# Half of the taps of a depthwise convolution as column-tiled matmuls on shifted copies

## The chip, the cores and the metric

The kernel runs on one core of a Trainium2 chip. The core has a tensor engine (PE; its weight loads are listed apart as PEld), a vector engine (DVE), a scalar engine (ACT), GpSimd (POOL) and a sync engine (SP), which here issues the DMA transfers. The engines work side by side, each through its own list of instructions in order, and wait for one another by semaphores. Operands lie in SBUF, 128 partitions wide; matmul results go to PSUM.

The metric is the device time of one execution in microseconds, as the median of several runs. The profile is one further execution recorded by the hardware profiler.

## The reference

Four layers over a stream of 512 latent tokens and 256 context tokens with 1024 channels, in fp32. Layer i uses mixer i mod 3: layers 0 and 3 a Conformer convolution, layer 1 a two-way RWKV-7 scan, layer 2 attention. Each layer normalises and modulates its input and adds its gated result to the stream. The part that matters:

```python
def conv_branch(h, w_in, dw, db, ln_g, ln_b, w_out):
    a, b, gate = jnp.split(h @ w_in, 3, axis=-1)
    y = a * jax.nn.sigmoid(b)
    y = depthwise_conv(y, dw, db)          # 31 taps, each channel for itself
    y = jax.nn.silu(layernorm(y, ln_g, ln_b))
    return (y * jax.nn.silu(gate)) @ w_out
```

`h @ w_in` is 1024 x 3072 and `w_out` 1024 x 1024. Layer 0 does this for context and latent tokens; layer 3, whose context result nobody reads, for the 512 latent tokens alone.

## The kernel before, in words

Data stand channel-major: a tile is 128 channels by all tokens, and there are NT = 8 channel tiles. In layer 0 context and latent lie in one padded row, so that a convolution yields 783 positions a tile; in layer 3 it yields 512.

**Projections.** A projection of one column tile is a product of 8 chunks of 128 channels, each as three fp32r products (`whi·hhi`, `whi·hlo`, `wlo·hhi`, L175 to L182), for segments of 512 and, in layer 0, 256 tokens. Weights come by `wload` (L153): a DMA of 512 KB on SP's queue (L157) into one of two raw buffers, ACT rounds them to `whi` (L166), and another engine takes the rest to `wlo` (L168). In the convolution layers that is GpSimd. Results go to a ring of PSUM buffers, three in layer 0 and six in layer 3.

**The loop.** For each tile m the kernel projects b and a, takes tanh of b on ACT (L319), forms the gated product `yp` on DVE (L326), and convolves (L333 to L343). Of the 31 taps ACT does the first with the bias into `Y`, ACT makes the products of 4 to 8 further ones that GpSimd adds up in `a2` (L335 to L339), and DVE does the other 22 to 26, one multiply-add over the tile each (L341); at last `a2` is added (L343). After each projection two steps of a filler run: the modulation of layers 0 to 2, weight columns by DMA, groups of four 128x32 matmuls (L198) that stand side by side in the columns of the array, and small turning matmuls (L205).

**Behind the loop.** Gate projections and the layernorm's sums alternate in a fixed order (`GATE_ORDER`): silu on ACT (L353), the result to DRAM (L354), and matmuls with a matrix of 1/1024 for the channel mean of `Y` and of its square (L362, L364). Then come mean and deviation (L380 to L384) and for each tile subtraction on GpSimd (L392), three passes on DVE (L393, L396, L398) and two on ACT, and the output projection in eight columns, whose results DVE adds to the stream (L413).

**What sets the order.** The program is written tile by tile; a scheduler that simulates a timeline by its own costs fixes each engine's order beforehand. The scan of layer 1 has an order written out by hand, and is not touched.

Of the kernel before, what the change touches and what calls it, by code (L numbers as in the profile page):

```python
# [80 lines left out]
class Trunk:  # L81
# [14 lines left out]
    conv_names = ("dw_0", "conv_db", "conv_ln_g", "conv_ln_b")  # L96
# [75 lines left out]
    def mm3(self, segs, w, x, kt, m0=0, m=P, k0=0, first=True, last=True):  # L172
        """segs: [(psum ap, token slice)]; psum += w[:, k, m0:m0+m]^T x[k0 + k][:, tokens]"""
# [54 lines left out]
    def stat_add(self, m, s):  # L228
        """squares of channel tile m: the first tiles added up by GpSimd, the last two by the tensor engine"""
# [14 lines left out]
    def table(self, func, after):  # L244
        """the scalar engine's table for func, loaded as soon as the column `after` is there"""
# [22 lines left out]
    def normed(self, i, R, segs):  # L268
        """hi/lo of h = x*R*gs + shift"""
# [13 lines left out]
    # ---- Conformer convolution layer  # L283
    def conv_layer(self, i, j, lat_only, filler):
        nc, tc, I = self.nc, self.tc, self.I
        segs = self.segs_of(lat_only)
        lo_t = CTX if lat_only else 0
        ntok = TOK - lo_t
# [6 lines left out]
        # padded positions: ctx at PAD.., latent at PAD+CTX+PAD..; latent only: PAD..  # L295
# [1647 lines left out]
```

## Time and profile before

| | |
|---|---|
| median of 3 runs | 2635.33 us (2633.45 to 2638.43) |
| span of the profiled execution | 2633.3 us; its time outside the span is not recorded apart |
| PE, DVE, GpSimd, ACT busy | 2287.3, 1766.8, 1203.3, 1170.2 us |
| layer 0: first projection, end of the gates, end of the output | 42.9, 411.7, about 490 us |
| layer 3: first projection, last sum, end | 2304.9, 2556.4, 2633.3 us |
| DVE taps (L341), both layers | 364 of 1451 ns, 506.6 us |
| GpSimd adds of taps (L339), both layers | 100 of 2082 ns, 208.2 us |

The views used below: busy time of each engine in stretches of the span, with the clock that TensorE was granted; groups of instructions by line and shape, with count, busy time, mean duration and what ended the idle time before them; and the timeline of one engine, whose rows are start, duration, engine, line, operation, result and operands, and the number of instructions that the row holds. A matmul of fp32 over 512 positions shows as two records.

### The profile page before, as it was taken

What the parts mean: (1) busy time and instruction counts of PE and PEld (TensorE: products, weight loads), DVE (VectorE), ACT (ScalarE), POOL (GpSimd) and SP (SyncE); (2) the same over time, 40 slices, a digit from 0 to 9 for tenths busy, and PEclk for the clock granted to TensorE, in tenths of its full rate; (3) what the DMA queues carried; (4) which work ended last, traced back from release to release, by engine and by line L of the source; (5) the groups of instructions that cost most, each with busy time, mean ns of one, the idle gap of its engine ahead of it and who ended that gap; (6) DMA issues with size and microseconds to landing.
All of it is one profiled execution on the core that took longest, in us unless ns stands there. A gap on an engine that the chain in (4) does not pass through costs nothing. (4 is left out here: it accounts for less than half of the span.)

```text
span 2633.3 us, 42476 instructions
## 1 busy us (share of the span) xinstructions
PE 2287.3 (87%) x15987; PEld 1787.2 (68%) x15987; DVE 1766.8 (67%) x2839; ACT 1170.2 (44%) x2672; POOL 1203.3 (46%) x1116
## 2 busy tenths in 40 slices
PE   6976879699998798898988999989999999877637
PEld 4755558476667566566666677988899998765425
DVE  3899996778345777777776452546454555689993
ACT  4433335334344455565544543456455454433432
POOL 1565755534144445555531104445454444457652
PEclk9988889799999878898885799999999999998769
DMA  7543314245976544354431473111111112212212
GB/s 256 168 147 117 126 68 147 60 123 160 317 249 195 154 101 104 96 119 123 109 79 39 155 226 99 42 41 49 49 57 57 57 49 67 65 48 64 76 52 80
DMA packets 351421, 288.95 MB, mean 110 GB/s; under 512 B 106136, under 2 KB 301040, under 8 KB 351216
## 3 DMA queue, kind: packets, MB, share of 16 engines
q1 hardware_dynamic: 351216, 286.24, 36.6%
q8 instruction: 126, 2.06, 0.3%
q14 instruction: 79, 0.65, 0.1%
HBM read 222.11 MB, written 57.77 MB: 106 GB/s over the span
## 5 line engine op out<-in xcount | busy, mean ns | idle before, releaser
L168 POOL TENSOR_TENSOR wlo<-wraw,whi 128x1024 fp32r<-128x1024 f32 x136 | 362.6, 2670 | 331.3 <-ACT whi L166 285.5
L341 DVE SCALAR_TENSOR_TENSOR Y<-yp,VC,Y 128x783 f32<-128x783 f32 (+1 forms) x364 | 506.6, 1451 | 4.8 <-ACT Y L333 3.5
L166 ACT ACTIVATE whi<-wraw 128x1024 fp32r<-128x1024 f32 x168 | 176.3, 1052 | 211.9 <-DMA wraw<-in_attn_w_in_dram 42.6
L339 POOL TENSOR_TENSOR a<-a,a 128x783 f32<-128x783 f32 (+1 forms) x100 | 208.2, 2082 | 75.5 <-ACT a L335 64.6
L179 PE MATMUL cps<-hhi,whi 128*128 128x512 f32 x576 | 187.7, 383 | 33.3 <-ACT sg L353 15.1
L179 PE MATMUL cps<-hhi,wlo 128*128 128x512 f32 x576 | 185.1, 375 | 21.5 <-POOL wlo L168 21.5
L1696 PE MATMUL pj<-whi,hhi 128*128 128x256 f32 x640 | 182.6, 286 | 4.2 <-ACT junk L1705 2.6
L179 PE MATMUL cps<-hlo,whi 128*128 128x512 f32 (+1 forms) x576 | 185.0, 376 | 0.0
L1696 PE MATMUL pj<-wlo,hhi 128*128 128x256 f32 x640 | 182.0, 285 | 0.0
L1696 PE MATMUL pj<-whi,hlo 128*128 128x256 f32 x640 | 181.9, 285 | 0.0
L1207 POOL TENSOR_SCALAR SD<-VT,DC 64x64 f32<-64x64 f32 x160 | 66.2, 414 | 226.9 <-DVE VT L1230 183.2
L179 PEld LDWEIGHTS cps<-hhi,whi 128*128 128x128 f32 x576 | 102.5, 203 | 71.2 <-ACT sg L353 18.8
L1007 PE MATMUL pg<-ARP,BK 128*128 128x256 f32 x384 | 147.8, 480 | 3.0 <-DVE BK L991 2.6
L338 ACT ACTIVATE a<-yp,VC 128x783 f32<-128x783 f32 (+1 forms) x100 | 83.0, 834 | 120.5 <-POOL a L339 120.4
L179 PEld LDWEIGHTS cps<-hhi,wlo 128*128 128x128 f32 x576 | 102.1, 201 | 43.0 <-POOL wlo L168 23.6
L1696 PEld LDWEIGHTS pj<-whi,hhi 128*128 128x128 f32 x640 | 123.6, 193 | 5.4 <-ACT junk L1705 3.3
L1696 PEld LDWEIGHTS pj<-wlo,hhi 128*128 128x128 f32 x640 | 123.7, 193 | 0.7
L1696 PEld LDWEIGHTS pj<-whi,hlo 128*128 128x128 f32 x640 | 123.4, 193 | 0.1
L1230 DVE SCALAR_TENSOR_TENSOR VT<-c,DC,SD 64x64 f32<-64x64 f32 x320 | 90.2, 282 | 49.3 <-PE c L1218 25.8
L1112 DVE TENSOR_TENSOR tm<-inst,Ti 96x207 f32<-96x207 f32 (+10 forms) x240 | 105.1, 438 | 18.6 <-DMA inst<-gn 10.7
L179 PEld LDWEIGHTS cps<-hlo,whi 128*128 128x128 f32 x576 | 102.4, 202 | 21.8 <-issue 2.4
L921 ACT ACTIVATE VT<-c 64x64 f32<-64x64 f32 x384 | 83.3, 217 | 73.0 <-PE c L1211 65.3
(342 smaller groups left out, 6234.4 us busy)
## 6 DMA issues: line engine op xcount, KB each, us to landing
mraw<-in_mod_w_dram SPq DMA_DIRECT2D x36, 1024.0 KB
wraw<-in_conv_w_in_dram SPq DMA_DIRECT2D x48, 512.0 KB
wraw<-in_attn_w_in_dram SPq DMA_DIRECT2D x48, 512.0 KB
mraw<-in_mod_w_dram SPq DMA_DIRECT2D x24, 512.0 KB
F<-dF SPq DMA_DIRECT2D x24, 384.0 KB
KR<-dF SPq DMA_DIRECT2D x24, 384.0 KB
wraw<-in_conv_w_out_dram SPq DMA_DIRECT2D x16, 512.0 KB
wraw<-in_attn_w_out_dram SPq DMA_DIRECT2D x16, 512.0 KB
```

What stands on the lines that cost most here:

```text
L166: nc.scalar.activation(hi[:, :n], raw[:, :n], AF.Copy)
L168: lo_eng.tensor_tensor(out=lo[:, :n], in0=raw[:, :n], in1=hi.bitcast(F32)[:, :n], op=ALU.subtract)
L179: nc.tensor.matmul(ps, a[:, k, m0:m0 + m], b[k0 + k][:, ts], start=first and k == 0 and i == 0, stop=last and k == kt - 1 and i == 2)
L338: nc.scalar.activation(a3, yp[:, w_:w_ + nout], AF.Copy, scale=tap(w_))
L339: nc.gpsimd.tensor_tensor(out=a2, in0=a2, in1=a3, op=ALU.add)
L341: nc.vector.scalar_tensor_tensor(out=y, in0=yp[:, w_:w_ + nout], scalar=tap(w_), in1=y, op0=ALU.mult, op1=ALU.add)
L921: nc.scalar.activation(out, in_, AF.Copy)
L1007: nc.tensor.matmul(pg[u - u % 2][:, u % 2, :], BK[:, u].rearrange("p s t -> p (s t)"), ARP[:, :, u, :], start=True, stop=True)
L1112: eng("im", j).tensor_tensor(out=o, in0=inst[0:96, j, j + 1:32].unsqueeze(2).to_broadcast([96, n, c]), in1=Ti[0:96, j, 0:c].unsqueeze(1).t ...
L1207: eng("SD", 2 * d + k).tensor_scalar(out=SD[own], in0=src, scalar1=dc[own], scalar2=0.0, op0=ALU.mult, op1=ALU.add)
L1230: nc.vector.scalar_tensor_tensor(out=S, in0=pc[own, 2, :], scalar=dc[own], in1=SD[own], op0=ALU.mult, op1=ALU.add)
L1696: nc.tensor.matmul(o[:, n, :], a, b[:, k, :], start=kh == 0 and k == 0 and e == 0 and n == 0, stop=kh == 1 and k == 3 and e == 2 and n == 1)
```

## The change

Only the two convolution layers change, and the helpers that they call.

- `PE_TAPS = 16`: taps 0 to 15 are done on PE. `yp` of a tile is copied into `X` by 16 DMAs of 32 partitions on SP's queue, so that row 32g + r of chunk n holds channel 32n + r shifted by g. `W` holds the taps as diagonal weights; DVE makes it per tile as a product with four stacked unit matrices (`eye4`). `convolve` sums, for each chunk of 32 channels, four matmuls of K = 128 and M = 32 into that chunk's 32 PSUM partitions. `X` has one buffer.
- DVE keeps 14 taps a tile; tap 16 with the bias is ACT's. DVE adds the PSUM result to `Y` and keeps running sums of `Y` and its square, which two matmuls a segment average at the end.
- GpSimd adds nothing any more; all `wlo` splits of these layers are on DVE.
- Each gate projection stands inside the loop: b and a of tile m, the convolution of tile m - 1, the gate of tile m - 2.
- All normalising passes but ACT's are on DVE, and the first output columns are multiplied chunk by chunk while the tiles are normalised.

```diff
-GATE_ORDER = "g0 s0 s1 g1 s2 s3 g2 s4 g3 s5 g4 s6 g5 s7 g6 g7".split()
-POOL_TAPS = (8, 8, 8, 8, 8, 8, 6, 4)
+PE_TAPS = 16
+FIRST = 2
...
+        osegs = [(s, (olat if s == 0 else 0), t0, n) for s, t0, n in segs]
+        nq, nv = PE_TAPS // 4, CW - PE_TAPS
+        xw = nout + PE_TAPS - 4
...
+        for m in range(NT):
+            order += [("b", m), ("a", m)] + [("c", m - 1)] * (m > 0) + [("g", m - 2)] * (m > 1)
+        order += [("c", NT - 1), ("g", NT - 2), ("g", NT - 1)]
...
-                w = self.wload(w_in[:, part * D + m * P: part * D + (m + 1) * P], NT, P, nc.gpsimd)
...
+                w = ws.pop(0)
+                if cols[len(done) + 1:]:
+                    ws.append(self.wload(cols[len(done) + 1], NT, P, nc.vector))
...
-                yp = cv.tile([P, max(width, TOK)], F32, tag="yp", name="yp", bufs=3)
...
+                y = yp[m] = cv.tile([P, max(width, TOK)], F32, tag="yp", name="yp", bufs=2)
...
-                nc.scalar.activation(y, yp[:, 0:nout], AF.Identity, scale=tap(0), bias=bias)
-                a2 = cv.tile([P, nout], F32, tag="a2", name="a2")
-                nc.scalar.activation(a2, yp[:, 1:1 + nout], AF.Copy, scale=tap(1))
-                for w_ in range(2, 1 + npool):
-                    a3 = cv.tile([P, nout], F32, tag="a3", name="a3", bufs=2)
-                    nc.scalar.activation(a3, yp[:, w_:w_ + nout], AF.Copy, scale=tap(w_))
-                    nc.gpsimd.tensor_tensor(out=a2, in0=a2, in1=a3, op=ALU.add)
-                for w_ in range(1 + npool, CW):
-                    nc.vector.scalar_tensor_tensor(out=y, in0=yp[:, w_:w_ + nout], scalar=tap(w_), in1=y,
-                                                   op0=ALU.mult, op1=ALU.add)
-                nc.vector.tensor_tensor(out=y, in0=y, in1=a2, op=ALU.add)
+                X[m] = cv.tile([P, 4, xw], F32, tag="X", name="X")
+                for n in range(4):
+                    for g in range(4):
+                        nc.sync.dma_start(X[m][32 * g:32 * g + 32, n, :], y[32 * n:32 * n + 32, g:g + xw])
+                nc.scalar.activation(Y[m], y[:, PE_TAPS:PE_TAPS + nout], AF.Identity,
+                                     scale=self.vec("dw", nv)[:, m:m + 1], bias=self.vec("conv_db")[:, m:m + 1])
+                w = W[m] = cv.tile([P, nq, 4, 32], F32, tag="W", name="W", bufs=2)
+                nc.vector.tensor_tensor(out=w, in0=self.eye4.unsqueeze(1).unsqueeze(1).to_broadcast([P, nq, 4, 32]),
+                                        in1=self.WT.rearrange("p (q r) -> p q r", q=nq)[:, :, 4 * m:4 * m + 4].unsqueeze(3)
+                                        .to_broadcast([P, nq, 4, 32]), op=ALU.mult)
+                for v in range(1, nv):
+                    taps.append(lambda v=v: nc.vector.scalar_tensor_tensor(
+                        out=Y[m], in0=y[:, PE_TAPS + v:PE_TAPS + v + nout], scalar=self.vec("dw", nv)[:, v * NT + m:v * NT + m + 1],
+                        in1=Y[m], op0=ALU.mult, op1=ALU.add))
...
+            def convolve(m):
+                self.mark(f"L{i}conv")
+                p = self.big("yps")
+                for q in range(nq):
+                    for s, o, t0, n in osegs:
+                        for c in range(4):
+                            nc.tensor.matmul(p[32 * c:32 * c + 32, 512 * s:512 * s + n], W[m][:, q, c, :],
+                                             X[m][:, c, o + 4 * q:o + 4 * q + n], start=q == 0, stop=q == nq - 1)
+                def add():
+                    for s, o, t0, n in osegs:
+                        nc.vector.tensor_tensor(out=Y[m][:, o:o + n], in0=p[:, 512 * s:512 * s + n], in1=Y[m][:, o:o + n], op=ALU.add)
...
+                        nc.vector.tensor_tensor(out=sums[0], in0=sums[0], in1=Y[m], op=ALU.add)
+                        nc.vector.tensor_tensor(out=sums[1], in0=sums[1], in1=sq, op=ALU.add)
...
-                    nc.gpsimd.tensor_tensor(out=z[:, t0:t0 + n], in0=Y[m][:, o:o + n], in1=mean[:, c0:c0 + n], op=ALU.subtract)
...
+                    nc.vector.tensor_tensor(out=zz, in0=Y[m][:, o:o + n], in1=mean[:, c], op=ALU.subtract)
...
-            w = self.wload(w_out[:, m * P:(m + 1) * P], NT, P, nc.gpsimd)
...
+        load = lambda m: self.wload(w_out[:, m * P:(m + 1) * P], NT, P, nc.vector)
+        first = [(load(m), self.big("ops")) for m in range(FIRST)]
+        for k in range(NT):
+            make(k)
+            for w, ps in first:
+                self.mm3([(ps[:, 512 * s:512 * s + n], slice(t0, t0 + n)) for s, t0, n in segs], [a[:, k:k + 1] for a in w],
+                         ([y[0][k]], [y[1][k]]), 1, first=k == 0, last=k == NT - 1)
```

What stands where on the engines after the change, at three places. In a row the name ahead of the arrow is the result, those behind it the operands, numbered as the program makes them; line numbers are the changed kernel's (L188 is a projection matmul, L382 a convolution's, L207 and L214 the modulation's, L177 a split, L372 a tap, L166 a weight load, L364 a copy to X).

PE in layer 0, after the projection of a for tile 3 (`cps_1273`): the convolution of tile 2 (`X_1058`).

```order
L188 MATMUL cps_1273<-hhi_120,wlo_1195 128x512
L188 MATMUL cps_1273<-hhi_120,wlo_1195 128x256
L207 MATMUL mps_1254<-mraw_1322,sc_75 32x512 x4
L382 MATMUL yps_1371<-X_1058,W_1076 32x512 x4
L382 MATMUL yps_1371<-X_1058,W_1076 32x256 x4
L382 MATMUL yps_1371<-X_1058,W_1076 32x512 x4
L382 MATMUL yps_1371<-X_1058,W_1076 32x256 x4
L214 MATMUL mps_1330<-pick_77,mrow_1328 128x2 x4
```

Eight groups of four short matmuls a tile, four sets of taps by two segments, are new on PE there; they stand together, with steps of the modulation among them.

DVE in layer 0, first before, then after, from the gated product of a tile on (`Y1` to `Y3` are the tiles' sums, `VC` the taps).

```order
L326 SCALAR_TENSOR_TENSOR yp_1228<-th_1226,cps_1162 128x512
L326 SCALAR_TENSOR_TENSOR yp_1228<-th_1226,cps_1162 128x256
L341 SCALAR_TENSOR_TENSOR Y1_501<-yp_840,VC_409,Y1_501 128x783
L207 TENSOR_TENSOR modT1_68<-mps_1213,VT_78 128x8
L341 SCALAR_TENSOR_TENSOR Y2_502<-yp_1035,VC_409,Y2_502 128x783
L341 SCALAR_TENSOR_TENSOR Y1_501<-yp_840,VC_409,Y1_501 128x783
L341 SCALAR_TENSOR_TENSOR Y3_503<-yp_1228,VC_409,Y3_503 128x783
```
```order
L177 TENSOR_TENSOR wlo_1408<-wraw_1404,whi_1406 128x1024
L359 SCALAR_TENSOR_TENSOR yp_1345<-th_1343,cps_1273 128x512
L359 SCALAR_TENSOR_TENSOR yp_1345<-th_1343,cps_1273 128x256
L177 TENSOR_TENSOR wlo_1490<-wraw_1486,whi_1488 128x1024
L372 SCALAR_TENSOR_TENSOR Y3_509<-yp_1345,VC_411,Y3_509 128x783 x2
L216 TENSOR_TENSOR modT1_68<-mps_1330,VT_79 128x8
L372 SCALAR_TENSOR_TENSOR Y3_509<-yp_1345,VC_411,Y3_509 128x783
L220 SCALAR_TENSOR_TENSOR gs1_72<-modT1_68,VT_79 128x8
L372 SCALAR_TENSOR_TENSOR Y3_509<-yp_1345,VC_411,Y3_509 128x783 x2
L368 TENSOR_TENSOR W_1663<-eye4_78,WT_431 128x512
L386 TENSOR_TENSOR Y2_508<-yps_1371,Y2_508 128x512
```

Before, the taps of up to three tiles wait in DVE's list at once; after, those of one, with splits, a weight product and the add from PSUM between them.

SP in layer 3 (`X_23224` is tile 2's copy, `X_23382` tile 3's; the `wraw` rows are weight loads, SGD1 the store of a gate).

```order
L364 DMA X_23224<-yp_23220 32x524 x16
L166 DMA wraw_23499<-in_conv_w_in_dram 128x8x128
L166 DMA wraw_23579<-in_conv_w_in_dram 128x8x128
L404 DMA SGD1_22916<-sg_23459 128x512
L166 DMA wraw_23622<-in_conv_w_in_dram 128x8x128
L364 DMA X_23382<-yp_23378 32x524 x16
L166 DMA wraw_23659<-in_conv_w_in_dram 128x8x128
```

Sixteen copies a tile stand in SP's list between the weight loads, where before there were loads and stores of gates alone. On PE the convolution of a tile of layer 3 is split: three single matmuls of L382 between projection matmuls, then thirteen together.

More of the change, by code (lines that the diff above doesn't have):

```diff
@@ L303, in conv_layer @@
             Y = [cv.tile([P, nout], F32, name=f"Y{m}", tag=f"Y{m}") for m in range(NT)]
-            hx = self.hx
-            nn = 512 + (0 if lat_only else CTX)
-            def project(part, m):
-                w = self.wload(w_in[:, part * D + m * P: part * D + (m + 1) * P], NT, P, nc.gpsimd)
-                ps = self.big("cps")
-                self.mm3([(ps[:, 512 * s:512 * s + n], slice(t0, t0 + n)) for s, t0, n in segs], w, hx, NT)
+            sums = [cv.tile([P, nout], F32, name="sum0"), self.tp.tile([P, 783], F32, tag="acc", name="sum1", bufs=1)[:, :nout]]
@@ new lines, in glu, with total @@
+                for v in range(1, nv):
[5 more added lines that the diff above has]
+                p = self.big("yps")
+                for q in range(nq):
+                    for s, o, t0, n in osegs:
[5 more added lines that the diff above has]
+                        nc.vector.tensor_tensor(out=Y[m][:, o:o + n], in0=p[:, 512 * s:512 * s + n], in1=Y[m][:, o:o + n], op=ALU.add)
+                def total():
+                    sq = sums[1] if m == 0 else self.tp.tile([P, 783], F32, tag="sq", name="sqy")[:, :nout]
+                    nc.scalar.activation(sq, Y[m], AF.Square)
+                    if m == 0:
+                        nc.vector.tensor_copy(sums[0], Y[m])
+                    else:
+                        nc.vector.tensor_tensor(out=sums[0], in0=sums[0], in1=Y[m], op=ALU.add)
+                        nc.vector.tensor_tensor(out=sums[1], in0=sums[1], in1=sq, op=ALU.add)
+                taps.extend((add, total))
@@ L354, in gate @@
                 nc.sync.dma_start(SGD[m][:, lo_t:], sg[:, lo_t:])
                 return sg
-            def sums(m):
-                self.mark(f"L{i}ln")
-                sq = self.tp.tile([P, 783], F32, tag="sq", name="sqy")
-                nc.scalar.activation(sq[:, :nout], Y[m], AF.Square)
-                for s, o, t0, n in osegs:
-                    nc.tensor.matmul(pm[:, 512 * s:512 * s + n], self.mean_m, Y[m][:, o:o + n],
-                                     start=(m == 0), stop=(m == NT - 1))
-                    nc.tensor.matmul(pq[:, 512 * s:512 * s + n], self.mean_m, sq[:, o:o + n],
-                                     start=(m == 0), stop=(m == NT - 1))
@@ L367, in conv_layer @@
-            for x in GATE_ORDER:
-                if x[0] == "g":
-                    sg = gate(int(x[1:]))
-                else:
-                    sums(int(x[1:]))
+            for x, m in order:
+                if x == "c":
+                    convolve(m)
+                    if m == NT - 1:
+                        vector_work(len(taps))
+                    continue
+                project(x, m)
+                if x == "a":
+                    glu(m)
+                if x == "g":
+                    sg = gate(m)
@@ L403, in out_proj @@
+            self.out_proj(i, w_out, hx, segs, normalize)
+    def out_proj(self, i, w_out, y, segs, make):
         nc = self.nc
@@ L408, in out_proj, with finish @@
         late = []
-        def part(m, ps, w, segs):
-            self.mm3([(ps[:, 512 * s:512 * s + n], slice(t0, t0 + n)) for s, t0, n in segs], w, y, NT)
+        def finish(m, ps, segs):
             for s, t0, n in segs:
@@ L417, in part @@
                     self.stat_add(m, s)
-        for m in range(NT):
-            w = self.wload(w_out[:, m * P:(m + 1) * P], NT, P, nc.gpsimd)
+        def part(m, ps, w, segs):
+            self.mm3([(ps[:, 512 * s:512 * s + n], slice(t0, t0 + n)) for s, t0, n in segs], w, y, NT)
+            finish(m, ps, segs)
+        load = lambda m: self.wload(w_out[:, m * P:(m + 1) * P], NT, P, nc.vector)
[5 more added lines that the diff above has]
+                         ([y[0][k]], [y[1][k]]), 1, first=k == 0, last=k == NT - 1)
+        ahead = [load(m) for m in range(FIRST, FIRST + 1)]
+        for m, (w, ps) in enumerate(first):
+            finish(m, ps, segs)
+        for m in range(FIRST, NT):
+            w = ahead.pop(0)
+            if m + 1 < NT:
+                ahead.append(load(m + 1))
             ps = self.big("ops")
```

119 lines of the change are left out of this document (68 added, 51 removed).

## The prediction, as it was put on record

> **What bounds the kernel now.** I began with the page's busy times: no engine fills the span, and the chain of waits has only two trivial pieces, so it decides nothing. Next came busy time by stretch, laid over the two convolution layers (columns: length; PE, PEld, DVE, ACT, POOL busy; granted clock, DMA share, GB/s). The four rows of the second fence are layer 0, the one of the third is the middle of layer 3's loop.
>
> ```profile
> span 2633.3 us, 42476 instructions
> PE 2287.3 (87%) x15987; PEld 1787.2 (68%) x15987; DVE 1766.8 (67%) x2839; ACT 1170.2 (44%) x2672; POOL 1203.3 (46%) x1116
> ```
> ```profile
> 42.90:76.00 33.10, 31.53 (x195) 23.28 (x199) 16.89 (x38) 12.29 (x21) 1.99 (x10) 1.00 0.61 205
> ...
> 200.00:300.00 100.00, 70.11 (x370) 51.73 (x368) 100.00 (x75) 30.50 (x35) 58.77 (x31) 0.83 0.36 116
> ...
> 386.20:411.70 25.50, 25.50 (x146) 22.11 (x145) 20.30 (x17) 14.17 (x20) 14.93 (x12) 1.00 0.45 141
> ...
> 437.00:490.00 53.00, 50.75 (x278) 42.55 (x276) 14.67 (x28) 14.90 (x25) 25.08 (x33) 1.00 0.35 115
> ```
> ```profile
> 2400.00:2500.00 100.00, 66.89 (x213) 47.65 (x212) 100.00 (x88) 38.54 (x54) 67.38 (x42) 0.81 0.22 66
> ```
>
> In both loops DVE is busy for the whole stretch while PE is idle for a third of it at a granted clock near 0.8. Only at the end of layer 0's loop, where the last gate projections run, is PE the full one. So the taps on DVE set the loops. The groups of instructions say what a tap costs, and DVE's timeline says why:
>
> ```profile
> L341 DVE SCALAR_TENSOR_TENSOR Y<-yp,VC,Y 128x783 f32<-128x783 f32 x182 | 289.0, 1645 | 1.8 <-ACT Y L333 1.1
> L341 DVE SCALAR_TENSOR_TENSOR Y<-yp,VC,Y 128x512 f32<-128x512 f32 x182 | 217.6, 1258 | 3.0 <-ACT Y L333 2.4
> L343 DVE TENSOR_TENSOR Y<-Y,a 128x512 f32<-128x512 f32 x8 | 5.4, 680 | 0.1
> ```
> ```profile
> 119.70 8.58 DVE L341 SCALAR_TENSOR_TENSOR Y<-yp,VC,Y 128x783 f32<-128x783 f32 x9
> 128.20 0.97 DVE L343 TENSOR_TENSOR Y<-Y,a 128x783 f32<-128x783 f32 x1
> ...
> 130.01 9.92 DVE L341 SCALAR_TENSOR_TENSOR Y<-yp,VC,Y 128x783 f32<-128x783 f32 x4
> ...
> 2358.55 12.66 DVE L341 SCALAR_TENSOR_TENSOR Y<-yp,VC,Y 128x512 f32<-128x512 f32 x19
> ```
>
> The mean tap is 1.65 us in layer 0 and 1.26 in layer 3, but some runs of taps cost 0.95 (8.58/9) and 0.67 (12.66/19), others 2.5 (9.92/4). I read the difference as DVE sharing with GpSimd's adds and splits; the change takes both off GpSimd.
>
> **The change on DVE.** The price of a `wlo` split there stands in the rows of line 168, since some already run on DVE:
>
> ```profile
> L168 DVE TENSOR_TENSOR wlo<-wraw,whi x32: 1210/1225/2873, 544.3 to 1580.4; 128x1024 fp32r<-128x1024 f32 x32
> ```
>
> A tile of layer 0 is now 14 taps x 0.95 = 13.3 us, three splits 3.7, the gated product, the add from PSUM and two running sums about 1.0 each (0.97 in the row of 128.20), the weight product W 0.7 (680 ns, L343 at 512): 21.7 us. In layer 3 it is 14 x 0.67 + 3.7 + five operations of 0.68 = 16.5 us. If taps kept today's contended means, these would be 31.5 and 24.7 us.
>
> **The change on PE.** The convolution is new: groups of four 128x32 matmuls, each on its own 32 columns. Groups of that form exist today in the modulation (x8 is one group of four, two records each):
>
> ```profile
> 111.59 0.52 PE L179 MATMUL cps<-hhi,wlo 128*128 128x512 f32 x2
> 112.05 1.06 PE L198 MATMUL mps<-mraw,sc 128*32 128x512 f32 x8
> ...
> 113.49 0.51 PE L179 MATMUL cps<-hlo,whi 128*128 128x512 f32 x2
> 113.84 0.51 PE L179 MATMUL cps<-hhi,wlo 128*128 128x512 f32 x2
> ...
> 126.88 1.92 PE L198 MATMUL mps<-mraw,sc 128*32 128x512 f32 x16
> 128.73 0.62 PE L179 MATMUL cps<-hhi,whi 128*128 128x512 f32 x2
> ...
> 653.24 0.64 PE L198 MATMUL mps<-mraw,sc 128*32 128x256 f32 x8 [0.68 <-DMA mraw<-in_mod_w_dram]
> 653.81 1.12 PE L789 MATMUL pa<-AL,A 64*128 64x512 f32 x2
> ...
> 384.58 1.05 PE L364 MATMUL pq<-sqy,mean_m 128*128 128x512 f32 x2
> 385.46 0.59 PE L362 MATMUL pm<-Y,mean_m 128*128 128x256 f32 x2
> 385.89 0.59 PE L364 MATMUL pq<-sqy,mean_m 128*128 128x256 f32 x2
> ```
>
> From start to start: a projection pair (512 + 256 positions) is 0.35 us (113.49 to 113.84). A 512-wide group, back to back, is 0.93 ((128.73 - 126.88)/2), a 256-wide one 0.57. One group alone between projections is 1.2 (111.59 to 113.49 less two pairs), so a switch in and out costs 0.27. One full-array fp32 matmul of 512 is 0.88 (384.58 to 385.46), of 256 0.43. Four column tiles thus take about the time of one.
>
> By the Trainium skill, "TensorE: Matmul & The Clock Gate", section "Measured speedup vs the span model", three column tiles of 512 run 2.38 times as fast as in turn, 0.79 of the ideal; at that rate a group would be 1.11 us and the sum below 11 us longer. The row of 0.93 disagrees, so I keep the row.
>
> Layer 0, from 42.9: the rest of PE's work is modulation:
>
> ```profile
> L198 PE MATMUL mps<-mraw,sc 128*32 128x512 f32 x256 | 35.2, 644 | 0.4 <-DMA mraw<-in_mod_w_dram 0.4
> L205 PE MATMUL mps<-pick,mrow 128*128 128x2 f32 x136 | 21.9, 282 | 53.3 <-ACT mrow L202 43.7 <-DVE modT L207 9.2 <-DVE xl L1579 0.4
> ```
>
> 24 projections x 24 pairs x 0.35 = 201.6 us; 256/8 = 32 groups x 1.2 = 38.4; 136/8 = 17 turning groups at the 0.9 of other groups of eight fp32 records = 15 (their busy time today, much of it after a wait, is 21.9); convolutions 8 x (4 x (0.93 + 0.57) + 0.3) = 50. Sum 305 us, 38 per tile, against DVE's 21.7: PE becomes the bound, even if the contention stayed (31.5). For stalls I take 10 us (estimate): between none (386.20 row: 25.5 busy of 25.5) and 5% (42.90 row: 1.57 idle of 33.1). All gates then end at 42.9 + 315 = 358, today at 411.7.
>
> Behind it lies the layernorm, today partly beside the gates:
>
> ```profile
> 386.73 1.19 DVE L381 TENSOR_TENSOR rs<-pq,m 128x512 f32<-128x512 f32 x2 [3.09 <-ACT m L380]
> ...
> 389.80 4.96 DVE L384 RECIPROCAL rs<-rs 128x512 f32<-128x512 f32 x2 [1.89 <-ACT rs L382]
> ...
> 433.69 0.96 DVE L398 TENSOR_TENSOR hlo<-z,hhi 128x768 fp32r<-128x768 f32 x1 [0.91 <-ACT hhi L397]
> ...
> 2556.43 0.69 DVE L381 TENSOR_TENSOR rs<-pq,m 128x512 f32<-128x512 f32 x1 [3.94 <-PE pq L364]
> ...
> 2585.19 2.07 DVE L413 SCALAR_TENSOR_TENSOR xl<-ops,modT,xl 128x512 f32<-128x512 f32 x3 [2.16 <-PE ops L179]
> ```
>
> Mean matmuls, subtraction, root and reciprocal take 11 us (385.46 to 394.76 with 2 for matmuls), then 8 tiles x 4 passes of 0.95 to 1.1 = 33 us, all on DVE: the last `hlo` at 358 + 44 = 402, today 434.7. Three output columns run chunk by chunk under those 33 us (3 x 8.4 = 25); five remain, as in today's 437 to 490. Layer 0 gives 32 us. If nothing covered the first three columns, 25 of these go.
>
> Layer 3, whose projection pace is
>
> ```profile
> 2304.91 1.65 PE L179 MATMUL cps<-hhi,whi 128*128 128x512 f32 x3 [5.79 <-ACT hhi L278]
> ...
> 2313.19 0.39 PE L179 MATMUL cps<-hhi,wlo 128*128 128x512 f32 x1
> 2313.42 0.39 PE L179 MATMUL cps<-hlo,whi 128*128 128x512 f32 x1
> ```
>
> 0.2275 us (0.23 in these two rows): 24 x 24 x 0.2275 = 131 us. The order splits a convolution: three single column matmuls among the projections, then 13. I price a lone one at the full 0.88 + 0.2, between 0.23 (if it ran like one of a group) and 1.2; with 13/4 x 0.93 + 0.3 this is 6.5 us a tile, 52 in all. 183 us, plus 7 for the slow start and stalls, ends the loop at 2304.9 + 190 = 2495. The subtraction of L381 follows at about 2501 (last add, sums, mean matmuls), today 2556.4. Today 28.8 us lie between it and the first add to the stream (L413); after the change 4.9 us to the end of the reciprocal, 8 x 4 passes of 0.68 = 21.8 and 2.2 of PE make 28.9, so the part that GpSimd did costs DVE nothing on balance: without its contention the other passes shrink. The output columns stay. With 1.5 us of doubt, layer 3 gives 54 us.
>
> The new transfers fill X by 16 DMAs a tile on SP's queue, behind the weight loads, and X has one buffer: a refill starts when the previous convolution has ended. Nearest rows, two small DMAs on chip and the longest wait of such an issue:
>
> ```profile
> 826.81 0.42 SPq L1044 DMA_DIRECT2D gn<-GM  x1
> 827.28 0.43 SPq L1043 DMA_DIRECT2D gw<-GM  x1
> SPq L1045 <- DMA gn<-GM: 11.8, 26, 2.0
> ```
>
> 16 x 0.47 = 7.5 us of issue and 2.0 to land: 9.5 us. In layer 0 some 31 us of projections lie between two convolutions, in layer 3 45 matmuls (10.2 us) to the first chunk and 70 (16 us) to the last. I take it as hidden; the other bound is below. Behind a waiting refill SP holds the weight loads of the projections after the next, so a late refill would also delay PE's operands there. On DVE a `wlo` can stand behind six taps, 5.7 us in layer 0 and 4.0 in layer 3, while the projection that covers it lasts 8.4 and 5.5 us: it costs nothing, and up to 24 x 1.2 = 29 us in layer 3 if the cover were gone by one split.
>
> Together 32 + 54 = 86 us. The span, 2633.3, is 2.0 below the median of the runs; from the median 2635.3 - 86 = **2549 us**.
>
> **Rivals.**
>
> Transfers bound in layer 3. A tile moves 128 x 4 x 524 x 4 bytes = 1.07 MB besides 1.5 MB of weights. The page's mean is
>
> ```profile
> DMA packets 351421, 288.95 MB, mean 110 GB/s; under 512 B 106136, under 2 KB 301040, under 8 KB 351216
> ```
>
> and at 110 GB/s a refill takes 10 us alone and 20 with a weight load each side of it, 4 us past the last chunk's 16, seven times, so +28 us or less: 2575. For it: short packets of 2 KB. Against: 205 GB/s in the 42.90 row.
>
> Slower than before: the 16 transfers of a refill take turns instead of overlapping. At 2.0 us each that is 32 us, 16 more than layer 3 hides, x 7 = +112, and about 1 x 7 in layer 0: 2549 + 119 = 2668. It decides from a refill of 16 + 86/7 = 28 us. Against: the rows show issues 0.47 apart, and waits of 2.0 are the longest of 26.
>
> The column tiles don't run side by side, so the change doesn't do what it says. A group is then 4 x 0.88 = 3.5 and 4 x 0.43 = 1.7 us: +8 x 4 x (2.6 + 1.15) = 120 in layer 0 and 8 x 3.25 x 2.6 = 68 in layer 3: 2737. The rows of L198 speak against it; only that X and W are other operands is for it.
>
> A larger gain: lone matmuls at 0.3 instead of 1.08 (8 x 3 x 0.78 = 19), no stalls (17): 2513.
>
> **How the numbers follow.** Forecast 0.68, transfer-bound 0.13, larger gain 0.09, turns 0.05, column tiles in turn 0.02, a gain lost to several waits so that nothing is seen 0.03. Price errors of the forecast: -36 as in the larger gain, +17 if every group pays its switch (8 x 8 x 0.27), +15 for stalls at 5% of 488 us. The range goes from 2508 to 2594, the upper end holding the transfer case and both upper bounds in part. A difference of 0.2% (5 us) is what a measurement here can tell. Faster 0.90, same 0.03, slower 0.07.
>
> **What would show it.** Right: no GpSimd adds; taps near 0.95 and 0.67; PE nearly full in layer 0's loop at a clock near 1.0; the last gate near 358; the subtraction of L381 near 2501 less layer 0's 32, that is 2469; L382 groups of x8 near 0.93. Wrong: PE waiting on DMA for X in layer 3, groups above 1.2 us, taps above 1.2, PE waiting on DVE's `wlo` queued behind taps.

## The result, and the profile after

The changed kernel takes 2539.4 us (median of four runs, 2535.4 to 2544.1) against 2634.4 us (2632.9 to 2638.4) before: a ratio of 0.9633, with a 95% interval of 0.9616 to 0.9649. The prediction was 2549 us. The span of its profiled execution is 2539.6 us, 93.7 less than before's 2633.3.

Four points of the timelines divide the span: the first projection of layer 0, layer 1's first memset, the first projection of layer 3, and the end.

| us | before | after | difference | predicted |
|---|---|---|---|---|
| layer 0, first projection to layer 1 | 443.6 | 391.2 | -52.4 | -32 |
| layers 1 and 2 | 1818.4 | 1830.1 | +11.7 | 0 |
| layer 3, first projection to the end | 328.4 | 274.6 | -53.8 | -54 |

Busy time by stretch of the changed kernel shows PE as the bound of both loops; the columns are as before (length; PE, PEld, DVE, ACT, POOL; clock, DMA share, GB/s).

```profile
120.00:200.00 80.00, 80.00 (x583) 56.75 (x576) 51.40 (x63) 18.36 (x23) 0.58 (x9) 1.00 0.75 221
200.00:300.00 100.00, 100.00 (x675) 74.52 (x674) 59.01 (x71) 20.28 (x27) 0.38 (x6) 1.00 0.71 209
300.00:343.50 43.50, 43.50 (x300) 29.27 (x299) 24.35 (x28) 8.13 (x12) 0.00 (x0) 1.00 0.40 111
343.50:384.20 40.70, 26.16 (x129) 20.91 (x128) 37.43 (x53) 24.60 (x31) 0.00 (x0) 0.83 0.26 81
...
2350.00:2400.00 50.00, 50.00 (x229) 30.58 (x222) 35.68 (x48) 11.66 (x15) 0.31 (x4) 1.00 0.42 111
...
2463.00:2489.00 26.00, 16.48 (x60) 12.55 (x61) 24.68 (x34) 13.64 (x20) 0.00 (x0) 0.80 0.20 61
```

In the stretch from 200 to 300 PE was busy for 70 us at a clock of 0.83 before and is busy for all 100 now, at full clock, while DVE went from 100 to 59. GpSimd has nothing left but memsets. Two stretches where DVE is the fuller engine remain: 343.5 to 384.2 and 2463 to 2489, the layernorm behind each loop.

The groups of the taps, layer 0 and layer 3, and the timeline of PE around a convolution of each layer:

```profile
L372 DVE SCALAR_TENSOR_TENSOR Y<-yp,VC,Y 128x783 f32<-128x783 f32 x112 | 114.8, 1033 | 4.5 <-ACT Y L365 2.3
```
```profile
L372 DVE SCALAR_TENSOR_TENSOR Y<-yp,VC,Y 128x512 f32<-128x512 f32 x112 | 82.0, 749 | 3.7 <-ACT Y L365 1.9
L382 PE MATMUL yps<-X,W 128*32 128x512 f32 x256 | 50.4, 600 | 3.9 <-DMA X<-yp 3.9
```
```profile
265.87 2.76 PE L382 MATMUL yps<-X,W 128*32 128x512 f32 x32
268.56 1.05 PE L214 MATMUL mps<-pick,mrow 128*128 128x2 f32 x8
...
2326.26 3.62 PE L382 MATMUL yps<-X,W 128*32 128x512 f32 x26
2329.81 0.51 PE L188 MATMUL cps<-hhi,wlo 128*128 128x512 f32 x1
...
2336.80 0.40 PE L188 MATMUL cps<-hhi,wlo 128*128 128x512 f32 x1
2337.13 1.04 PE L382 MATMUL yps<-X,W 128*32 128x512 f32 x2
2338.10 0.50 PE L188 MATMUL cps<-hhi,whi 128*128 128x512 f32 x1
2338.44 0.39 PE L188 MATMUL cps<-hlo,whi 128*128 128x512 f32 x1
```

Busy time over count gives 1.02 us a tap in layer 0 (114.8/112) and 0.73 in layer 3 (82.0/112), where it was 1.59 (289.0/182) and 1.20 (217.6/182); the signs that the prediction named were 0.95 and 0.67. In layer 0 two groups of 512 and two of 256 take 2.69 us (265.87 to 268.56), 1.34 a pair. In layer 3 a single column matmul keeps the next projection matmul 0.97 us away (2337.13 to 2338.10), as long as a whole group, and the projection's steps ahead of it (2336.80 to 2337.13) and behind it are 0.33 and 0.34 instead of 0.23 long. That makes 1.2 us for one. The thirteen column matmuls that three single ones leave behind take 3.55 us (2326.26 to 2329.81).

The layernorm's rows on DVE, a refill of X on SP's queue, and the longer of PE's two waits for X in layer 3 (for another tile than that refill's):

```profile
345.65 0.69 DVE L431 TENSOR_TENSOR rs<-ln,m 128x512 f32<-128x512 f32 x1
...
382.26 1.90 DVE L448 TENSOR_TENSOR hlo<-ring,hhi 128x768 fp32r<-128x768 f32 x2
...
2463.05 0.69 DVE L431 TENSOR_TENSOR rs<-ln,m 128x512 f32<-128x512 f32 x1 [1.48 <-PE ln L428]
```
```profile
2329.95 10.01 SPq L364 DMA_DIRECT2D X<-yp  x16
```
```profile
2311.76 1.57 PE L382 MATMUL yps<-X,W 128*32 128x512 f32 x2 [3.15 <-DMA X<-yp]
```

The subtraction that stood at 386.7 stands at 345.7, the one at 2556.4 at 2463.1. Sixteen copies take 10.0 us of SP, 0.63 us each instead of the 0.47 that I had taken.

### The profile page after: what moved, and what is told of

Same layout as the page of the kernel before. It is cut to its first block, busy times and chain, and to the rows that moved or that the text cites. A ratio compares the mean times of both kernels' runs of the same rounds, so it can differ in the third digit from the quotient of the medians.

```text
span 2539.6 us, 43974 instructions
## 1 busy us (share of the span) xinstructions
PE 2318.8 (91%) x16671; PEld 1773.1 (70%) x16671; DVE 1562.3 (62%) x2842; ACT 1082.5 (43%) x2556; POOL 780.5 (31%) x928
## 5 line engine op out<-in xcount | busy, mean ns | idle before, releaser
L177 POOL TENSOR_TENSOR wlo<-wraw,whi 128x1024 fp32r<-128x1024 f32 x72 | 173.4, 2411 | 193.5 <-ACT whi L175 170.8
L372 DVE SCALAR_TENSOR_TENSOR Y<-yp,VC,Y 128x783 f32<-128x783 f32 (+1 forms) x224 | 196.8, 891 | 8.1 <-ACT Y L365 4.2
L177 DVE TENSOR_TENSOR wlo<-wraw,whi 128x1024 fp32r<-128x1024 f32 x96 | 122.1, 1273 | 111.3 <-ACT whi L175 109.4
L188 PE MATMUL cps<-hhi,whi 128*128 128x512 f32 x576 | 179.7, 369 | 3.3 <-ACT hhi L287 3.3
L188 PE MATMUL cps<-hlo,whi 128*128 128x512 f32 (+1 forms) x576 | 176.7, 360 | 0.0
L188 PE MATMUL cps<-hhi,wlo 128*128 128x512 f32 (+1 forms) x576 | 176.6, 360 | 0.0
L188 PEld LDWEIGHTS cps<-hhi,whi 128*128 128x128 f32 x576 | 97.1, 191 | 49.3 <-issue 17.5
L188 PE MATMUL ops<-hhi,whi 128*128 128x512 f32 (+1 forms) x320 | 103.9, 366 | 26.7 <-ACT hhi L447 23.3
L1181 DVE TENSOR_TENSOR Ti<-Ti,tm 96x31 f32<-96x31 f32 (+15 forms) x248 | 110.4, 445 | 5.8 <-POOL tm L1178 0.2
```

The lines of the kernel that those rows point to most:

```text
L177: lo_eng.tensor_tensor(out=lo[:, :n], in0=raw[:, :n], in1=hi.bitcast(F32)[:, :n], op=ALU.subtract)
L188: nc.tensor.matmul(ps, a[:, k, m0:m0 + m], b[k0 + k][:, ts], start=first and k == 0 and i == 0, stop=last and k == kt - 1 and i == 2)
L372: taps.append(lambda v=v: nc.vector.scalar_tensor_tensor(out=Y[m], in0=y[:, PE_TAPS + v:PE_TAPS + v + nout], scalar=self.vec("dw", nv)[:, ...
L1181: eng("ia", j).tensor_tensor(out=Ti[0:96, j + 1:32, 0:c], in0=Ti[0:96, j + 1:32, 0:c], in1=o, op=ALU.add)
```

## The experiments

My theory at this point: DVE set both loops before, its taps stretched by GpSimd's work beside them (A); the change takes that work away and moves half of the taps, and PE is now the bound. The main rival: the taps were slow for reasons of their own, and the gain comes from their leaving DVE (B). I call one kernel faster or slower than another where the intervals of their ratios lie apart. Each kernel ran beside the kernel before on the same chip, whose medians there were 2636 to 2642 us. The parts of their profiled executions, cut as above:

| kernel | median us | ratio to before, 95% interval | layer 0 | layers 1, 2 | layer 3 |
|---|---|---|---|---|---|
| before, again | 2638.0 (one run) | | 444.9 | 1820.7 | 328.5 |
| changed, again | 2539.1 (one run) | | 390.7 | 1829.4 | 274.8 |
| e1 nothing on GpSimd, no taps on PE | 2568.5 | 0.9733 (0.9703 to 0.9762) | 409.0 | 1823.8 | 289.6 |
| e2 splits on GpSimd | 2535.1 | 0.9615 (0.9589 to 0.9641) | 395.3 | 1826.7 | 264.8 |
| e3 gates last | 2543.6 | 0.9644 (0.9618 to 0.9669) | 379.3 | 1825.9 | 289.5 |
| e4 12 taps on PE | 2535.0 | 0.9612 (0.9586 to 0.9637) | 383.1 | 1832.2 | 279.1 |
| e5 two buffers for X in layer 3 | 2526.1 | 0.9568 (0.9541 to 0.9595) | 390.2 | 1819.2 | 263.1 |
| e6 e3 with 12 taps and two X buffers | 2515.5 | 0.9525 (0.9503 to 0.9547) | 374.2 | 1832.9 | 264.7 |
| e7 e6 with 16 taps and half the gates inside in layer 3 | 2510.6 | 0.9518 (0.9496 to 0.9540) | 372.5 | 1834.0 | 260.6 |
| e8 4 taps on PE | 2599.2 | 0.9859 (0.9837 to 0.9882) | 410.0 | 1826.2 | 316.2 |
| e9 e6 with the X copies on GpSimd's queue | 2535.4 | 0.9621 (0.9603 to 0.9638) | 404.3 | 1823.2 | 258.3 |

### e1: the contention alone

The kernel before, with GpSimd's work in the convolution layers given to DVE. With its adds go the products that ACT made for them (50 a layer):

```diff
-POOL_TAPS = (8, 8, 8, 8, 8, 8, 6, 4)
+POOL_TAPS = (1, 1, 1, 1, 1, 1, 1, 1)
...
-                w = self.wload(w_in[:, part * D + m * P: part * D + (m + 1) * P], NT, P, nc.gpsimd)
+                w = self.wload(w_in[:, part * D + m * P: part * D + (m + 1) * P], NT, P, nc.vector)
...
-                    nc.gpsimd.tensor_tensor(out=z[:, t0:t0 + n], in0=Y[m][:, o:o + n], in1=mean[:, c0:c0 + n], op=ALU.subtract)
+                    nc.vector.tensor_tensor(out=z[:, t0:t0 + n], in0=Y[m][:, o:o + n], in1=mean[:, c0:c0 + n], op=ALU.subtract)
...
-            w = self.wload(w_out[:, m * P:(m + 1) * P], NT, P, nc.gpsimd)
+            w = self.wload(w_out[:, m * P:(m + 1) * P], NT, P, nc.vector)
```

> The kernel before with nothing but memsets on GpSimd in the convolution layers: ACT does taps 0 and 1, DVE the other 29, all splits and the subtraction of the normalising. No tap on PE, gates still behind the loop. Theory A (DVE was the bound, and GpSimd's work beside it stretched its taps from 0.95 and 0.67 us to 1.65 and 1.26): taps go to 0.95 and 0.67, a tile of layer 0 costs DVE 29 x 0.95 + 1.0 + 1.0 + 2 x 1.22 = 32 us instead of 43, of layer 3 24 instead of 31; layer 0 ends some 60 us and layer 3 some 50 us earlier, about 2530 in all, so that removing the contention alone is worth about as much as the whole change. Theory B (taps are slow for reasons of their own and the change gains because half of them left DVE): taps stay near 1.6 and 1.25, DVE has six more of them, and the time rises by 40 us or more, to 2680.

Measured: 2568.5 us, a ratio of 0.9733, some 70 us less than before with *more* work on the engine that was full. The groups of taps of the two layers, the first tanh of layer 0 in ACT's timeline, and a stretch of layer 0:

```profile
L341 DVE SCALAR_TENSOR_TENSOR Y<-yp,VC,Y 128x783 f32<-128x783 f32 x232 | 223.7, 1028 | 2.3 <-ACT Y L333 1.9
```
```profile
L341 DVE SCALAR_TENSOR_TENSOR Y<-yp,VC,Y 128x512 f32<-128x512 f32 x232 | 156.6, 741 | 0.7 <-ACT Y L333 0.6
```
```profile
77.65 0.81 ACT L319 ACTIVATE th<-cps 128x768 f32<-128x768 f32 x1
```
```profile
200.00:300.00 100.00, 80.84 (x394) 57.59 (x393) 96.20 (x111) 21.25 (x26) 0.57 (x9) 0.83 0.30 98
```

232 taps take 223.7 us where 182 took 289.0: 0.96 us each, and 0.675 in layer 3, the prices of theory A. B falls. By the Trainium skill ("SBUF — State Buffer", "Who interferes with whom") a DVE instruction with two inputs in SBUF contends with a GpSimd instruction that reads SBUF; a tap has two, `yp` and `Y`, and the rows agree. That it is GpSimd and not ACT's products, which are gone here too, e2 shows below. But 2568 is also 38 us above what I expected of A: my sum made DVE full from the first projection on, at 44.9. It has no tap to do before the first tanh at 77.7, and afterwards it is at 96 of 100, not at 100; the subtraction behind the loop stands at 365.1, where 32 us a tile from 44.9 on would give 301. Half of that gap is the start, which my sum by engine did not contain. So of the change's 97 us (2634.4 x 0.0367) some 70 could be had without a single tap on PE. The taps on PE, the gates inside the loop and the first output columns add some 26 us together to that; they were not taken apart by one run each. These are not shares of the gain: with the taps on PE, e2 finds that part of GpSimd's work can come back for nothing.

### e2: the contention put back in part

```diff
-            ws = [self.wload(cols[0], NT, P, nc.vector)]
+            ws = [self.wload(cols[0], NT, P, nc.gpsimd)]
...
-                    ws.append(self.wload(cols[len(done) + 1], NT, P, nc.vector))
+                    ws.append(self.wload(cols[len(done) + 1], NT, P, nc.gpsimd))
```

> The changed kernel with the splits of the 24 input projections back on GpSimd in both convolution layers; all else as changed. Theory A: taps beside a split cost 2.5 us instead of 0.95 again, so the mean tap rises to some 1.3 us in layer 0, but DVE has 16 us a tile to spare there and 6 in layer 3 and gives 3.7 us of splits away: the time stays within 6 us of the changed kernel's 2539. If DVE were still the bound of the loops it would rise by 3 to 6 us a tile, 25 to 90 us in all.

Measured: 2535.1 us, the same as the changed kernel within what these runs can tell. The taps (layer 0, layer 3) did slow down:

```profile
L372 DVE SCALAR_TENSOR_TENSOR Y<-yp,VC,Y 128x783 f32<-128x783 f32 x112 | 133.2, 1192 | 18.0 <-ACT Y L365 15.4
```
```profile
L372 DVE SCALAR_TENSOR_TENSOR Y<-yp,VC,Y 128x512 f32<-128x512 f32 x112 | 104.4, 941 | 11.3 <-ACT Y L365 4.4 <-POOL wlo L177 4.2
```

1.19 and 0.93 us instead of 1.02 and 0.73, with nothing moved but the splits, so GpSimd's work stretches taps by itself. The time did not follow, but that does not show yet that DVE has slack, as I had meant it to. DVE also gave the splits away, 24 of 1.22 us a layer, and that is more than the 18 and 22 us by which the taps grew. In layer 0 it is busy for less of the time than in the changed kernel, where the same stretch has 134.8 us:

```profile
120.00:340.00 220.00, 216.95 (x1505) 153.37 (x1498) 126.82 (x143) 45.23 (x59) 39.26 (x28) 0.99 0.67 195
```

e4 is the better evidence for the slack. Layer 0 is 4 us longer, and layer 3 ten us *shorter*, which I had not expected. In that kernel's order three tiles of layer 3 have all their column matmuls in one piece, and eight single ones stand among the projections, where the changed kernel has no such tile and 17 single ones. That led to e5.

### e3 and e4: the order and the share

e3 moves the gate projections behind the last convolution and normalises beside them (of the edit only the order is shown):

```diff
-            order += [("b", m), ("a", m)] + [("c", m - 1)] * (m > 0) + [("g", m - 2)] * (m > 1)
-        order += [("c", NT - 1), ("g", NT - 2), ("g", NT - 1)]
+            order += [("b", m), ("a", m)] + [("c", m - 1)] * (m > 0)
+        order += [("c", NT - 1)] + [("g", m) for m in range(NT)]
...
```

> The changed kernel with the eight gate projections moved out of the loop, behind the last convolution; sums, mean, deviation and the normalising passes run on DVE and ACT beside them, in place, the gate is kept in SBUF, and only the last split waits for the last gate. Theory A (PE is the bound and its sum doesn't depend on the order, while 26 to 41 us of layernorm stand behind the loop with PE half idle): layer 0 ends 20 us and layer 3 about 12 us earlier, 2505 to 2512. Rival (the gates inside the loop fill time in which PE would wait for X or for DVE): the loops stretch by as much as the gates took, 5 to 10 us a tile, and the gain is gone or the kernel is slower than 2539.

Measured: 2543.6 us, no gain beyond the intervals. The parts say why: layer 0 is 12 us shorter, as the theory has it, if by less than its 20; layer 3 is 15 us longer. There PE waits for X, where the changed kernel waited 3.9 us in all:

```profile
PE yps L381 <- DMA X<-yp: 23.1, 9, 4.1
```

So both sides were right, one in each layer. With 783 positions two projections and the modulation cover a refill but for one wait of 5.9 us; with 512 they do not.

e4 gives four taps of each tile back to DVE:

```diff
-PE_TAPS = 16
+PE_TAPS = 12
...
```

> The changed kernel with 12 instead of 16 taps on PE: 18 taps a tile on DVE. Theory A (PE bound in both loops): layer 0 loses 8 x 1.32 = 11 us of PE time and layer 3 8 x 0.9 = 7, DVE's 3.8 and 2.7 us more a tile are hidden; 2521. If DVE bounds, it is 8 x (3.8 + 2.7) = 52 us slower, 2591; if neither bounds, no difference.

Measured: 2535.0 us, less than a third of the gain expected and within the intervals no different from the changed kernel. Layer 0 is 8.1 us shorter (391.2 to 383.1; 10.6 expected), as it must be if PE bounds it and DVE has room for 32 more taps: from 120 to 340 DVE is busy for 167.8 us instead of 134.8, PE still for 216.7 of 220. Layer 3 is 4.5 us longer instead of 7 shorter. Its convolutions take 46.1 us of PE instead of 50.4, so 4 us less and not 7, and PE waits 4.8 us for DVE's last sum, 1.5 before; so there PE's sum is not all that counts, and these two do not make the whole difference.

### e5: two buffers for X

```diff
-                X[m] = cv.tile([P, 4, xw], F32, tag="X", name="X")
+                X[m] = cv.tile([P, 4, xw], F32, tag="X", name="X", bufs=2 if lat_only else 1)
...
```

> The changed kernel with two buffers for X in layer 3 (layer 0 has no room): a refill no longer waits for the convolution before it, and the order then puts 16 column matmuls in one piece in six of the eight tiles instead of three single ones and 13. Theory A (PE is the bound of layer 3, and a single column matmul costs it some 1.2 us instead of 0.23): 18 fewer single ones give 15 to 17 us and the last waits for X 4 us more, 2520 to 2526. Rival (layer 3 is held by DVE or by the weights, the single ones stand in its gaps): within 5 us of the changed kernel.

Measured: 2526.1 us. Layer 3 takes 263.1 us instead of 274.6. Its convolutions on PE, one of them and the group:

```profile
2328.61 3.64 PE L382 MATMUL yps<-X,W 128*32 128x512 f32 x32
2332.18 0.51 PE L188 MATMUL cps<-hhi,whi 128*128 128x512 f32 x1
```
```profile
L382 PE MATMUL yps<-X,W 128*32 128x512 f32 x256 | 35.4, 596 | 0.0
```

The same 128 matmuls take 35.4 us of PE instead of 50.4: a tile in one piece is 3.64 us, where the split ones average 6.3 (50.4/8). I had counted 18 single ones fewer; the orders have 17 before and 6 now, but those in twos and threes cost more than their share too. And the thirteen behind three single ones saved nothing: they took 3.55 us (2326.26 to 2329.81 in the changed kernel), as long as sixteen do here (3.57, 2328.61 to 2332.18). 15 us less of PE and 3.9 of waits for X would make 19; 11.5 arrived. The four runs of this kernel lie between 2518.5 and 2533.2 us; the profiled one is the fastest, and 11 of the 22.9 us by which its span is shorter lie in layers 1 and 2, which the edit does not touch.

### e6, e7 and e9: put together

e6 joins e3, 12 taps and two X buffers.

```diff
-PE_TAPS = 16
+PE_TAPS = 12
...
+        order += [("c", NT - 1)] + [("g", m) for m in range(NT)]
...
+                X[m] = cv.tile([P, 4, xw], F32, tag="X", name="X", bufs=2 if lat_only else 1)
...
```

> Gates behind the loop as in the run with the gates last, 12 taps on PE, and two buffers for X in layer 3. Theory A: the gates-last order gained 12 us in layer 0 and lost 15 in layer 3 only because two projections do not cover a refill of the one X buffer; with two buffers layer 3 needs 131 us of projections, about 30 of convolutions and 5 for the slow start, with the layernorm beside the gates, so from its first projection to the end it takes about 235 us instead of 275; layer 0 gains 12 and 8 us: 2480 to 2490. Rival (DVE becomes the bound in layer 3 with 18 taps, 19 us a tile against PE's 15): layer 3 takes 250 us or more, 2500.

Measured: 2515.5 us. Layer 0 did nearly what was expected (374.2 us, 17 less than the changed kernel's; 20 expected), layer 3 did not (264.7 instead of 235). Its waits name weights and X:

```profile
ACT whi L175 <- DMA wraw<-in_conv_w_in_dram: 43.8, 11, 11.4
...
PE yps L381 <- DMA X<-yp: 10.7, 4, 7.3
```

I read these as SP's queue, whose 10 us of copies a tile stand ahead of weight loads. e9 is e6 with another queue for the copies:

```diff
-                        nc.sync.dma_start(X[m][32 * g:32 * g + 32, n, :], y[32 * n:32 * n + 32, g:g + xw])
+                        nc.gpsimd.dma_start(X[m][32 * g:32 * g + 32, n, :], y[32 * n:32 * n + 32, g:g + xw])
```

> The combined run with the X copies issued from GpSimd's queue instead of SP's. There a refill's 16 issues take 10 to 11 us of SP per tile (0.67 us each), weight loads stand behind them, and ACT waited 44 us for weights in layer 3. Theory A (SP's queue, not the transfers, held layer 3 of the combined run): the weight waits go away, layer 3 falls from 265 to 240 to 250 us and the kernel from 2515 to 2492 to 2502. Rival (the copies themselves are the limit, or GpSimd issues them no faster): layer 3 stays at 265 us or gets longer, 2515 or more.

Measured: 2535.4 us. The waits for weights left the list of layer 3, but it fell only to 258.3 us, and layer 0 grew by 30. On GpSimd's own list the copies of layer 0 now wait behind one another for PE:

```profile
POOL X L363 <- PE yps L381: 95.4, 6, 25.9
```

and the order that goes with it splits the convolutions of layer 0 as well, three single matmuls ahead of 21 in seven of its eight tiles. The issues themselves are faster there, 0.49 us each:

```profile
2299.82 7.90 POOL L363 DMA_DIRECT2D X<-yp  x16
```

My reading was at most a small part: SP's queue is worth 6 us in layer 3, not 15 to 25. I had passed over the rival that I had put on record for e6 myself, that DVE with its 18 taps a tile becomes the bound of layer 3. The middle of the loop in e6, in e9 and in e7 (below; 14 taps a tile on DVE there):

```profile
2270.00:2400.00 130.00, 114.51 (x485) 66.72 (x484) 119.33 (x173) 28.20 (x36) 0.91 (x12) 0.92 0.50 128
```
```profile
2320.00:2420.00 100.00, 88.03 (x397) 53.48 (x396) 99.50 (x147) 21.48 (x28) 48.13 (x108) 0.97 0.45 117
```
```profile
2300.00:2400.00 100.00, 100.00 (x498) 64.70 (x491) 83.33 (x113) 26.13 (x32) 0.61 (x8) 0.99 0.52 135
```

In e9 DVE is busy for 99.5 of 100 us and PE for 88; in e6 DVE is the fuller one too, 119 of 130 against 115. So the rows speak for that rival: the sum for e6 left DVE out. No run changes DVE's load there alone, so how much of the 30 us it accounts for stays open.

e7 keeps e6's layer 0 and gives layer 3 its 16 taps and every second gate back:

```diff
-PE_TAPS = 12
+PE_TAPS = (12, 16)
...
-            order += [("b", m), ("a", m)] + [("c", m - 1)] * (m > 0)
+            order += [("b", m), ("a", m)] + [("c", m - 1)] * (m > 0) + [("g", m // 2)] * (m % 2 and lat_only)
...
```

> Layer 0 as in the combined run (12 taps on PE, gates behind the loop); layer 3 with 16 taps on PE, two buffers for X, four gates inside the loop in every second tile and four behind it. Theory A: in the combined run layer 3 took 265 us because a tile without a gate is too short for SP's issues and transfers (ACT waited 44 us for weights, PE 11 us for X); with gates in every second tile PE's load is 17.3 us a tile against DVE's 16.5, and 22 us of gates cover the layernorm: layer 3 takes 245 to 250 us instead of 265, the kernel 2495 to 2503. Rival (DVE and PE are too evenly loaded, or SP still holds the loop): layer 3 stays at 260 to 265 us and the kernel at 2512.

Measured: 2510.6 us (2505.5 to 2512.5), 29 us below the changed kernel; it has the lowest median here, though its interval overlaps that of e6. Layer 3 is 260.6 us; the rival's figure. The layernorm's first row starts there at 2426.0, 9 us before the last gate's end at 2435.1, so that only a third of its 25 us is covered.

### e8: few taps on PE

```diff
-PE_TAPS = 16
+PE_TAPS = 4
...
```

> The changed kernel with only 4 taps on PE and 26 a tile on DVE, gates inside the loop, nothing on GpSimd. If PE bounds layer 0 with 16 taps, it loses three groups of each kind there, 8 x 3 x 1.32 = 32 us of PE time, and DVE comes to 33 us a tile, just below PE's 33.5: 24 to 30 us less in layer 0. In layer 3 DVE comes to 24.6 us a tile against PE's 21 and takes over: 5 to 12 us more. 2518 to 2525, better than with 16 taps. Rival (half of the taps must leave DVE for the gain): 2560 or more, near the run without PE taps at 2569.

Measured: 2599.2 us: wrong by 75, and on the rival's side. Taps cost 0.97 us (202.2/208), as before, so nothing is wrong with the prices. A stretch of layer 0 and the waits of layer 3:

```profile
120.00:200.00 80.00, 69.86 (x393) 51.02 (x386) 68.80 (x83) 16.54 (x21) 0.38 (x6) 0.87 0.73 216
...
300.00:370.00 70.00, 45.61 (x245) 33.80 (x243) 65.30 (x76) 15.21 (x24) 0.19 (x3) 0.85 0.32 89
```
```profile
PE yps L382 <- DMA X<-yp: 34.9, 5, 10.8
...
PE ln L428 <- DVE sum L394: 18.9, 1, 18.9
```

With PE at 33.5 and DVE at 33 us a tile, by the sums, neither has room. From 120 to 200 PE is busy for 70 of 80 us and DVE for 69; I read that as each waiting for the other. At the end of the loop no gates are left to cover DVE's last taps, and PE waits for the sums (18.9 us in layer 3, 17.7 in layer 0). e1, with no tap on PE at all and its gates behind the loop, is 31 us faster. Sixteen taps are more than the sums of work call for; my reading is that the slack pays. The order that the scheduler fixed for this kernel could be at fault as well, and no run tells the two apart.

### The two kernels once more

> The kernel before once more, for its profile: how long layers 1 and 2, which no change touches, take in another execution. They took 1818 us in the first profile and 1824 to 1832 in the profiles of the changed kernels. If that is the spread between executions, this one lies anywhere in 1815 to 1835; if the changed convolution layers lengthen them, it lies at 1818 again.

> The changed kernel once more, for its profile: layers 1 and 2 took 1830 us in the first. Spread between executions: anywhere in 1815 to 1835. A cost of the change: 1828 to 1832 again.

Layers 1 and 2 took 1818.4 and 1820.7 us in the two profiles of the kernel before, 1830.1 and 1829.4 in those of the changed one, though PE, DVE, ACT and GpSimd have the same lists there but for the last rows, and SP but for a few swaps. That looks like a cost of the change, but e5, which shares the changed kernel's lists for these layers, took 1819.2, and the other kernels lie between 1823 and 1834 without regard to what they change. With the same lists, then, two executions differ by 11 us. The lag comes in many pieces of 0.2 to 2 us, most of them in layer 2. So up to 15 us of any difference between two profiles here are not the convolution layers'. Where they come from was not found.

## Why the prediction was right, point by point

**What bound the kernel**: right. DVE's taps set both loops, and they were slow because of GpSimd's work beside them; e1 shows it by the tap prices and by the time, e2 by the tap prices with GpSimd's splits alone. I had put this in as a reading of a few rows and gave its removal no price of its own, although by itself it is worth 70 us. And one of these rows does not show what I took it for. Beside the 19 taps of 0.67 us from 2358.55 on GpSimd was not idle:

```profile
2350.03 2.81 POOL L168 TENSOR_TENSOR wlo<-wraw,whi 128x1024 fp32r<-128x1024 f32 x1
2361.11 15.69 POOL L168 TENSOR_TENSOR wlo<-wraw,whi 128x1024 fp32r<-128x1024 f32 x2 [8.27 <-ACT whi L166]
```

Two splits took 15.7 us there, of which the first alone took 12.9, where the one before took 2.8. So in this stretch GpSimd was held up and the taps were not; what decides which of the two waits, no run here shows. The price of 0.67 was right all the same: e1 has 0.675 with GpSimd idle.

**DVE no longer the bound**: right. DVE's busy share of the loop fell to 59 of 100 while PE's rose to 100, and e4 gave DVE 32 more taps in layer 0, which became shorter.

**Layer 0**: the mechanism was right, the size too small by 20 us of 52. The loop took 300.0 us (43.6 to 343.6) where the sum said 305 and 10 of stalls. The stalls were the step that failed: PE is busy for every microsecond from 120 to 343.5. The price of the groups gives the other 5: 1.34 us for a group of 512 with one of 256, not 1.50, times 32. Then the layernorm: 40.6 us from the last gate to the last `hlo` (384.2), not 44. The last 2 us are rounding (32.7 to 32) and the output columns.

**Layer 3**: right in sum (53.8 of 54 us), with errors that cancel, which is luck. The last convolution ended 194.4 us after the first projection, not 190. A single column matmul costs 1.2 us with the slow steps on both sides, not 1.08, and the thirteen behind three of them 3.55, not 13/4 x 0.93 = 3.0. Of the 7 us for the slow start and stalls, the waits for X alone took 3.9. Against that, the subtraction followed 3.6 us later, not 6, so that it stands 198 us after the first projection where I had 196, and the 1.5 us of doubt were not needed.

**The transfers of X**: right that they are hidden, within the 3.9 us. But 16 issues take 10 to 11 us of SP, not 7.5, and the margin was thin: e3, which took a third of the cover away, lost 23 us to them. The rival in which transfers take turns had the right place and the wrong size. The price of the single buffer was in my sum without my naming it: it made the order split the convolutions, and e5 got 11.5 us by a second one.

**Column tiles side by side**: right. Sixteen column matmuls in one piece take 3.64 us, 0.91 a group of four, against 0.88 for one full-array matmul of that length. At the rate that the Trainium skill ("TensorE: Matmul & The Clock Gate", "Measured speedup vs the span model") has for three column tiles, 2.38 times, it would by my estimate have been 1.11; the trace has 3.9 times for four tiles, better than that rate.

**The total**: 86 us predicted, 95 to 97 measured. 20 us too little in layer 0 stand against 12 us that layers 1 and 2 took longer in the profile, of which the prediction knew nothing. That the total came within 10 us is in part luck.

## What to carry to other kernels

Before moving work from a full engine to another, look whether that engine is slow because of a neighbour: compare the same instruction in stretches with and without the neighbour's work, and try the kernel with the neighbour idle. A sum of work by engine predicted the loops here when one engine was clearly the fuller one (16 taps), and failed by 75 us when two were level (4 taps), probably because then each wait is somebody's loss. A sum for one engine is not enough: e6 was forecast from PE's alone. And a buffer that is refilled while its last reader runs costs not only the wait: it made the order break one piece of work into short ones, each at the price of a whole group.

## What the runs showed of the hardware

One 128 x 32 matmul of 512 positions alone among full-width ones keeps PE for 0.97 us, as long as four of them side by side, and thirteen in a row take as long as sixteen (3.55 and 3.57 us). Taps of 783 positions cost DVE 0.96 us alone and 1.59 on average beside GpSimd's adds and splits, so that GpSimd's work in layer 0 cost DVE more than it took off it: 289.0 us for 182 taps beside it, 223.7 us for all 232 without. It can also be GpSimd that is held up: one split took 12.9 us beside taps that kept their 0.67. And of copies of 32 partitions SP issues one in 0.63 to 0.70 us in the changed kernel, GpSimd's queue one in 0.49.
